# PEER in a hybrid block: gathered activations for block 2, and a dense product that ends ahead of the loop

## The chip, the cores and the metric

The kernel runs on one core of a Trainium2 chip. The metric is the device time of the whole program in microseconds (us), as the median of several executions.

## The reference, cut to what matters

One layer for 512 tokens of width 1024, all in float32: a projection, sparse attention, a chunked DeltaNet and a merge give x. Then comes PEER, a mixture of 16384 experts of one neuron each, of which every token takes 8 heads x 16 = 128:

```
h2 = rms_norm(x, norm2_gain)
q = h2 @ w_query                          # 8 heads x 2 x 128
s = q . sub_keys                          # 2 x 128 scores a head
expert, best = top 16 of the 16 x 16 sums of the two top-16 lists
gate = softmax(best)
act[n, hk] = gelu(u[expert[n, hk]] . h2[n])
x[n] += sum over hk of gate[n, hk] * act[n, hk] * v[expert[n, hk]]
```

Tables u and v have 16384 rows of 1024 numbers each. An expert's number is 128 times its first key plus its second.

## The kernel before, in words

PEER handles the tokens in four blocks of 128. Block 3 (GATHERED) follows the formula: `gathered(s)` for s = 0 to 127 fetches, for each of the block's tokens, the row of its expert s by an indirect DMA on POOL (`uv` holds u and v side by side, so a row is 8 KB and one gather 1 MB), multiplies its u half with the token's h2 and sums it on DVE (L960), takes Gelu and gate on ACT, and adds the v half times that number to `x1g` on DVE (L963).

Blocks 0 to 2 (WHOLE, 384 columns) compute the activations of all 16384 experts instead. `dense_u(i)` takes tile i, 128 experts: it loads `ut` (512 KB), splits it into two fp32r parts, `uh` (a cast on ACT, L167) and `ul` (a subtraction on DVE, L168), and multiplies them with the two parts of h2 transposed (`hT`): 8 times three matmuls (`mm3`, L91) of 384 columns. Gelu goes on ACT. 42 of the results are spilled, each stored to DRAM (L819) and loaded again later (`gs`); the others stay (`ge`).

`choose(b)` picks block b's experts and gates on DVE. `spread(b)` turns them into gate matrices, an expert by token: for 8 tokens at a time DVE compares a row of numbers with the first keys (`oa`, one instruction, L983) and, token by token, with the second keys, times the gate (`ob`, L986); PE multiplies the two one-hot matrices of each token (`wo<-oa,ob`, two matmuls for one fp32 product); ACT copies the results into `gb` (L992); and for 16 tokens (TC) at a time 1 MB is stored to `gd` in DRAM, in pieces of 8 KB. There are 24 such stores.

In the last loop `dense_v(i)` takes tile i of table v: load `vt` (512 KB), split it (`vh` on ACT L1044, `vl` on DVE L1045), multiply the activations into the gates of the tile (`gt`, L1046; gates are loaded for 8 tiles (IC) at a time, 1.5 MB in pieces of 512 B), split the product into `ch` and `cl`, and add 6 x 2 x 3 / 2 = 18 matmuls of 512 columns into six accumulators (`acc`).

Each engine, and SP for its DMA queue, works through its instructions in one fixed order. That order comes from the program's text: 62 tiles of the dense product are put among `choose` and `spread`, by the count of pieces of `spread` that are done, and 66 in the loop, about one behind every second `dense_v`; 6 of block 3's gathers come early, and 122 follow in the loop in proportion to the work that was issued.

## Time and profile before

| | |
|---|---|
| median of 3 runs | 1843.3 us (1842.14 to 1844.12) |
| the profiled execution | 1844.26 us |
| its span in the trace | 1842.5 us |
| PE, DVE, ACT, POOL busy | 1791.8, 1442.0, 803.1, 188.6 us |
| DMA traffic | 396.74 MB |

The span runs from the first to the last instruction that the trace shows; the execution's own time has 1.8 us more. The stages, in the trace's own time: up to 680 us all that precedes PEER's choice, to 1028 us the choice and the gate products (the last `wo<-oa,ob` ends there), then the loop. PE is TensorE's matmuls, and their busy time is not the same as work at its peak; "DMA share" is the mean busy share of the core's 16 DMA engines.

### The profile page before, as it was taken

What the parts mean: (1) busy time and instruction counts of PE and PEld (TensorE: products, weight loads), DVE (VectorE), ACT (ScalarE), POOL (GpSimd) and SP (SyncE); (2) the same over time, 40 slices, a digit from 0 to 9 for tenths busy, and PEclk for the clock granted to TensorE, in tenths of its full rate; (3) what the DMA queues carried; (4) which work ended last, traced back from release to release, by engine and by line L of the source; (5) the groups of instructions that cost most, each with busy time, mean ns of one, the idle gap of its engine ahead of it and who ended that gap; (6) DMA issues with size and microseconds to landing.
All of it is one profiled execution on the core that took longest, in us unless ns stands there. A gap on an engine that the chain in (4) does not pass through costs nothing.

```text
span 1842.5 us, 26292 instructions
## 1 busy us (share of the span) xinstructions
PE 1791.8 (97%) x9527; PEld 1572.5 (85%) x9527; DVE 1442.0 (78%) x3291; ACT 803.1 (44%) x1401; POOL 188.6 (10%) x132
## 2 busy tenths in 40 slices
PE   5999999999999999999999999999999999999998
PEld 4787677878788899999999988888888888888887
DVE  5767988654667899999997686788787887787886
ACT  5433434443533334555655444344443444343442
POOL 0000000000000000010000112122121222212220
PEclk9999999999999999999999999999999999999999
DMA  4211111111643214567676898989988988898974
GB/s 148 92 64 63 58 41 58 52 52 41 211 147 130 89 52 142 186 226 258 250 268 228 307 365 305 336 316 361 337 313 327 347 315 309 335 357 313 343 299 170
DMA packets 142354, 396.74 MB, mean 215 GB/s; under 512 B 10704, under 2 KB 71760, under 8 KB 122768
## 3 DMA queue, kind: packets, MB, share of 16 engines
q1 hardware_dynamic: 123792, 260.84, 40.3%
...
## 4 chain that ended last, share of the span: by engine, by line
PE 82%; DVE 8%; DMA 6%; ACT 2%; issue 1%; SPq 0%; DVEq 0%; ACTq 0%
PE mm L91 28%; PE acc L91 25%; PE wo L91 6%; PE dn L91 5%; PE at L91 3%; DMA vt<-in_uv_dram 2%; DMA gt<-gd 2%; DVE ul L168 1%; DVE ob L986 1%; PE tr L91 1%; PE at L571 0%; PE dn L320 0%; DMA wt<-in_w_br_dram 0%; DVE tmp L229 0%; DVE gt L1046 0%
## 5 line engine op out<-in xcount | busy, mean ns | idle before, releaser
L91 PE MATMUL acc<-vl,ch 128*128 128x512 f32 x768 | 299.5, 390 | 1.1 <-DVE vl L1045 1.1
L91 PE MATMUL acc<-vh,cl 128*128 128x512 f32 x768 | 298.2, 389 | 0.0
L91 PE MATMUL acc<-vh,ch 128*128 128x512 f32 x768 | 263.1, 390 | 4.9 <-ACT vh L1044 4.9
L951 POOL DMA_INDIRECT row<-in_uv_dram,eidx x124 | 178.6, 1441 | 832.3 <-DVE x1g L963 775.1
L167 ACT CAST uh<-ut 128x1024 fp32r<-128x1024 f32 x128 | 134.6, 1051 | 150.0 <-PE mm L91 84.0
L1045 DVE TENSOR_TENSOR vl<-vt,vh 128x1024 fp32r<-128x1024 f32 x128 | 156.4, 1222 | 50.3 <-ACT vh L1044 47.6
L168 DVE TENSOR_TENSOR ul<-ut,uh 128x1024 fp32r<-128x1024 f32 x128 | 155.9, 1219 | 34.4 <-ACT uh L167 33.8
L91 PE MATMUL mm<-hTh,uh 128*128 128x384 f32 x496 | 168.6, 340 | 2.9 <-ACT gs L818 1.9
L91 PEld LDWEIGHTS acc<-vh,ch 128*128 128x128 f32 x768 | 143.3, 188 | 32.1 <-ACT vh L1044 6.6
L91 PE MATMUL mm<-hTh,ul 128*128 128x384 f32 x496 | 168.0, 340 | 2.7 <-DVE ul L168 2.7
L91 PEld LDWEIGHTS acc<-vl,ch 128*128 128x128 f32 x768 | 144.2, 188 | 30.2 <-DVE vl L1045 2.1
L963 DVE SCALAR_TENSOR_TENSOR x1g<-row,co,x1g 128x1024 f32<-128x1024 f32 x128 | 163.8, 1280 | 7.4 <-ACT co L962 5.3
L91 PEld LDWEIGHTS acc<-vh,cl 128*128 128x128 f32 x768 | 144.1, 188 | 29.2
L1044 ACT CAST vh<-vt 128x1024 fp32r<-128x1024 f32 x128 | 133.9, 1046 | 78.4 <-DMA vt<-in_uv_dram 64.0
L91 PE MATMUL mm<-hTl,uh 128*128 128x384 f32 x496 | 167.3, 337 | 0.0
L167 ACT CAST ch<-gt 128x384 fp32r<-128x384 f32 x128 | 65.5, 512 | 218.1 <-PE acc L91 211.1
L960 DVE CUSTOM_DVE_ANT_0 scr<-row,h2g 128x1024 f32<-128x1024 f32 x128 | 156.0, 1218 | 0.3
L91 PE MATMUL mm<-hh,wh 128*128 128x512 f32 x344 | 144.6, 424 | 3.6 <-ACT hh L167 2.1
L168 DVE TENSOR_TENSOR wl<-wt,wh 128x1024 fp32r<-128x1024 f32 (+1 forms) x81 | 90.1, 1115 | 63.4 <-ACT wh L167 63.2
L91 PE MATMUL mm<-hh,wl 128*128 128x512 f32 x344 | 137.3, 401 | 0.0
L91 PE MATMUL mm<-hl,wh 128*128 128x512 f32 x344 | 136.9, 398 | 0.0
L167 ACT CAST wh<-wt 128x1024 fp32r<-128x1024 f32 (+1 forms) x81 | 77.7, 962 | 110.9 <-PE mm L91 86.7
...
## 6 DMA issues: line engine op xcount, KB each, us to landing
ut<-in_uT_dram SPq DMA_DIRECT2D x128, 512.0 KB
vt<-in_uv_dram SPq DMA_DIRECT2D x128, 512.0 KB
...
sgd<-tmp SPq DMA_DIRECT2D x16, 256.0 KB
```

The costliest lines, as they stand in the source:

```text
L91: hop[0] = PE.matmul(o, l, r, start=start, stop=stop).ins
L167: S.copy(hi, src)
L168: return V.tensor_tensor(lo, src, hi.bitcast(F32), op=ALU.subtract).ins
L951: G.indirect_dma_start(out=row.rearrange("p t d -> p (t d)"), out_offset=None, in_=uv, in_offset=bass.IndirectOffsetOnAxis(ap=released.get ...
L960: V.tensor_tensor_reduce(scr, row[:, 0], h2g, 1.0, 0.0, op0=ALU.mult, op1=ALU.add, accum_out=a)
L963: V.scalar_tensor_tensor(x1g, row[:, 1], co, x1g, op0=ALU.mult, op1=ALU.add)
L986: V.tensor_scalar(ob[:, t], io, sl[:, 1, n:n + 1], sl[:, 2, n:n + 1], op0=ALU.is_equal, op1=ALU.mult)
L1044: S.copy(vh, vt)
L1045: paced = V.tensor_tensor(vl, vt, vh.bitcast(F32), op=ALU.subtract)
```

## The change

Block 2 (HALF) leaves the dense product, which keeps blocks 0 and 1 and so 256 columns. Its activations come from gathers of the u halves alone: `ask(s)` fetches 128 rows of 4 KB, and `products()` multiplies and sums them with the block's h2 on DVE, into one column of `act` each, 128 in all. Then Gelu runs over `act` and is multiplied into block 2's gates ahead of `spread(2)`, so that in the loop only the gates of blocks 0 and 1 are multiplied by activations. The V product keeps all three blocks.

All 128 tiles of the dense product now come ahead of the loop, placed by a running count of costs (`along`). 48 of them (i % 8 in NATIVE) go to PE unsplit: fp32 products straight from `ut` and an fp32 copy of h2 transposed (`hTf`), with no cast and no subtraction. Activations are stored and loaded in groups of four tiles, 28 of the 32 groups of 512 KB each. `ob` is one comparison for 8 tokens, as `oa` is, and the gate is multiplied in by ACT, token by token. `gd` is written in pieces of 512 B and read in pieces of 12 KB. 16 gathers of block 3 come early, beside `spread(2)`, and 112 stay in the loop. There are three `vt`.

```diff
-WHOLE, GATHERED = (0, 1, 2), 3
-NU = len(WHOLE) * P
+DENSE, HALF, GATHERED = (0, 1), 2, 3
+WHOLE = DENSE + (HALF,)
+NU = len(DENSE) * P
...
-AHEAD = 20
-KEPT = 42
-SPILLED = {i for i in range(P) if i * KEPT // P != (i + 1) * KEPT // P}
-EARLY = 6
-HEAD = 4, 4
-EARLY_FROM, EARLY_TO = 6, 20
+GE = 4
+ONCHIP = {0, 8, 16, 24}
+NATIVE = (1, 4, 6)
...
     def dense_u(i, a_):
-        ut = up.tile([P, 8, P], F32, name="ut", bufs=2)
+        ut = uw.tile([P, 8, P], F32, name="ut", bufs=2)
         load(ut, uT[i])
-        uh = up.tile([P, 8, P], F32R, name="uh", bufs=2)
-        ul = up.tile([P, 8, P], F32R, name="ul", bufs=2)
-        split(uh, ul, ut)
-        for k in range(8):
-            mm3(a_, (uh[:, k, :], ul[:, k, :]), (hT[0][:, k, :NU], hT[1][:, k, :NU]), k == 0, k == 7)
-        if i in SPILLED:
...
-            nc.sync.dma_start(gsd[i], ge)
+        if i % 8 in NATIVE:
+            for k in range(8):
+                mm(a_, ut[:, k, :], hTf[:, k, :], k == 0, k == 7)
         else:
-            ges[i] = up.tile([P, NU], F32, name="ge", bufs=AHEAD + 2)
-            S.activation(ges[i], a_, AF.Gelu)
+            uh = uw.tile([P, 8, P], F32R, name="uh", bufs=2)
+            ul = uw.tile([P, 8, P], F32R, name="ul", bufs=2)
+            split(uh, ul, ut)
+            for k in range(8):
+                mm3(a_, (uh[:, k, :], ul[:, k, :]), (hT[0][:, k, :NU], hT[1][:, k, :NU]), k == 0, k == 7)
+        g, r = divmod(i, GE)
+        if r == 0:
+            if g in ONCHIP:
+                ges[g] = up.tile([P, GE, NU], F32, name="ge", bufs=len(ONCHIP))
+            else:
+                ges[g] = up.tile([P, GE, NU], F32, name="gs", bufs=2)
+        S.activation(ges[g][:, r], a_, AF.Gelu)
+        if r == GE - 1 and g not in ONCHIP:
+            gsd[g] = dr.tile([P, GE * NU], F32, name=f"gs{g}")
+            nc.sync.dma_start(gsd[g], ges.pop(g).rearrange("p r n -> p (r n)"))
...
-    released = {}
+    uv2 = uv.rearrange("e (t d) -> (e t) d", t=2)
+    asked = []
+    def ask(s):
+        if s % 2 == 0:
+            asked.append(rowq.tile([P, 2, D], F32, name="row", bufs=ROWS))
+        G.indirect_dma_start(
+            out=asked[s // 2][:, s % 2],
+            out_offset=None,
+            in_=uv2,
+            in_offset=bass.IndirectOffsetOnAxis(ap=eidh[:, s:s + 1], axis=0),
+        )
+    def products():
+        for s in range(AHEAD):
+            ask(s)
+        for s in range(P):
+            if s + AHEAD < P:
+                ask(s + AHEAD)
+            r = asked[s // 2][:, s % 2]
+            V.tensor_tensor_reduce(r, r, h2h, 1.0, 0.0, op0=ALU.mult, op1=ALU.add, accum_out=act[:, s:s + 1])
+            yield
...
-    gd = dr.tile([NCH, P, P * TC], F32, name="gd")
+    gd = dr.tile([P // IC, P, NCH, IC * TC], F32, name="gd")
...
                 oa = gp.tile([P, TB, P], F32, name="oa", bufs=2)
                 ob = gp.tile([P, TB, P], F32, name="ob", bufs=2)
-                rows_ = sl[:, 0, n0:n0 + TB, None].to_broadcast([P, TB, P])
-                paced = V.tensor_tensor(oa, io[:, None].to_broadcast([P, TB, P]), rows_, op=ALU.is_equal)
+                for i, o_ in enumerate((oa, ob)):
+                    which = sl[:, i, n0:n0 + TB, None].to_broadcast([P, TB, P])
+                    V.tensor_tensor(o_, io[:, None].to_broadcast([P, TB, P]), which, op=ALU.is_equal)
                 for t in range(TB):
                     n = n0 + t
-                    V.tensor_scalar(ob[:, t], io, sl[:, 1, n:n + 1], sl[:, 2, n:n + 1], op0=ALU.is_equal, op1=ALU.mult)
+                    S.activation(ob[:, t], ob[:, t], AF.Copy, scale=sl[:, 2, n:n + 1])
...
-            nc.sync.dma_start(gd[b * (P // TC) + c], gb.rearrange("p i n -> p (i n)"))
-            yield paced
+            dst = gd[:, :, b * (P // TC) + c, :].rearrange("g p k -> p g k")
+            nc.sync.dma_start(dst, gb.rearrange("p (g i) n -> p g (i n)", i=IC))
+            yield
...
+    uw = pool(gx, "uw", reuse_waits="tile")
     gp = pool(gx, "gp", reuse_waits="tile")
-    todo = list(first)
-    def dense(left):
-        while len(todo) > left:
+    todo = list(range(P))
+    total_c = NB * C_CHOOSE + NCH * C_PIECE + P + EARLY * C_SUM
+    spent_c = [0]
+    def along(cost):
+        spent_c[0] += cost
+        while len(todo) > LAST and (P - len(todo)) * total_c < spent_c[0] * (P - LAST):
             dense_u(todo.pop(0), bank("mm")[:, :NU])
...
+    of_half, done_h = products(), 0
+    def some(n):
+        for _ in range(n):
+            if next(of_half, 0) is None:
+                along(1)
+    along(C_CHOOSE)
+    choose(HALF)
+    along(C_CHOOSE)
+    choose(GATHERED)
+    some(8)
     n, slot = 0, 0
-    dense(len(first) - HEAD[0])
-    choose(GATHERED)
-    dense(len(first) - HEAD[0] - HEAD[1])
-    rest = len(todo)
-    for b in WHOLE:
+    for b in DENSE:
+        along(C_CHOOSE)
         choose(b)
-        for paced in spread(b, gp):
+        some(8)
+        for _ in spread(b, gp):
             n += 1
-            dense(rest * (NCH - n) // NCH)
-            with tc.issue_after(paced.ins):
-                if len(released) < min(ROWS, EARLY):
-                    s = len(released)
-                    released[s] = rowq.tile([P, 1], I32, name="free", bufs=ROWS)
-                    V.tensor_copy(released[s], eidx[:, s:s + 1])
-                while slot < EARLY and slot * (EARLY_TO - EARLY_FROM) < (n - EARLY_FROM) * EARLY:
-                    gathered(slot)
-                    slot += 1
+            along(C_PIECE)
+            some((P - 24) * n // 16 - (P - 24) * (n - 1) // 16)
+    some(P)
+    S.activation(act, act, AF.Gelu)
+    V.tensor_tensor(flat(gate[HALF]), flat(gate[HALF]), act, op=ALU.mult)
+    for i, _ in enumerate(spread(HALF, gp)):
+        along(C_PIECE)
+        while slot * 8 < (i + 1) * EARLY:
+            gathered(slot)
+            along(C_SUM)
+            slot += 1
+    while todo:
+        dense_u(todo.pop(0), bank("mm")[:, :NU])
     gx.close()
     rx.close()
...
+    load_gates(0)
...
-        if i % IC == 0:
-            gt[0] = ex.tile([P, NCH, IC, TC], F32, name="gt", bufs=2)
-            load(gt[0].rearrange("p c i n -> p c (i n)"), gd.rearrange("c p k -> p c k")[:, :, i * TC:(i + IC) * TC])
-        g = gt[0][:, :, i % IC, :]
-        vt = ex.tile([P, D], F32, name="vt", bufs=2)
...
+        if i % IC == 1 and i + IC < P:
+            load_gates(i // IC + 1)
+        g = gts[i // IC][:, :, i % IC, :]
+        vt = ex.tile([P, D], F32, name="vt", bufs=3)
...
-        V.tensor_tensor(g, activations(i).rearrange("p (c n) -> p c n", n=TC), g, op=ALU.mult)
+        gdn = g[:, :ND]
+        V.tensor_tensor(gdn, activations(i).rearrange("p (c n) -> p c n", n=TC), gdn, op=ALU.mult)
...
-    late = fresh[AHEAD:]
-    total_u = len(late)
-    total = P * V_COST + total_u * U_COST
-    spent, slot = 0, EARLY
     for i in range(P):
         paced = dense_v(i)
-        spent += V_COST
-        if late and (total_u - len(late)) * (P - END) <= i * total_u:
-            dense_u(late.pop(0), ps3.tile([P, NU], F32, name="a_", bufs=2))
-            spent += U_COST
         with tc.issue_after(paced.ins):
-            while (slot - EARLY) * total < spent * (P - EARLY) and slot < P:
+            while (slot - EARLY) * P < (i + 1) * (P - EARLY) and slot < P:
                 gathered(slot)
                 slot += 1
     xs = [rowq.tile([P, 2, D], F32, name="xs", tag="row", bufs=ROWS)[:, 0] for b in WHOLE]
```

The order on DVE, where the last gate matrices give way to the loop. Before (`ul` belongs to a dense tile, `oa` and `ob` to the gates, and `gt`, `cl`, `vl` are the loop's first tile):

```order
L168 TENSOR_TENSOR ul<-ut,uh 128x1024 x2
L983 TENSOR_TENSOR oa<-io,sl 128x1024
L986 TENSOR_SCALAR ob<-io,sl 128x128 x8
L983 TENSOR_TENSOR oa<-io,sl 128x1024
L986 TENSOR_SCALAR ob<-io,sl 128x128 x8
L168 TENSOR_TENSOR ul<-ut,uh 128x1024 x4
L1046 TENSOR_TENSOR gt<-ge,gt 128x24x16 x6
L168 TENSOR_TENSOR cl<-gt,ch 128x384 x2
L1045 TENSOR_TENSOR vl<-vt,vh 128x1024
```

In the changed kernel, at the same place:

```order
L172 TENSOR_TENSOR ul<-ut,uh 128x1024
L1024 TENSOR_TENSOR oa<-io,sl 128x1024
L1024 TENSOR_TENSOR ob<-io,sl 128x1024
L172 TENSOR_TENSOR ul<-ut,uh 128x1024 x36
L1115 TENSOR_TENSOR gt<-ge,gt 128x16x16 x4
L1115 TENSOR_TENSOR gt<-gs,gt 128x16x16 x4
L172 TENSOR_TENSOR cl<-gt,ch 128x384 x2
L1112 TENSOR_TENSOR vl<-vt,vh 128x1024
L1000 ISA row,a<-row,h2g 128x1024
```

Behind the last `ob` there were 4 subtractions of dense tiles and then the loop; now there are 36. On PE, 53 dense tiles (33 split, 20 unsplit) now stand between the last `wo<-oa,ob` and the first `acc`, where 3 or 4 stood; of 80 split tiles 44 have their `ul` ahead of the last `ob`, where 60 had it before.

The order of SP's DMAs from the last stores of gates (`gd<-gb`) to the first tiles of table v (`vt`); `gs_9799<-gs` and its like are stores of spilled activations, `gs<-gs_6319` loads of them. Before:

```order
L819 DMA gs_9834<-gs 128x384
L102 DMA ut<-in_uT_dram 128x1024
L993 DMA gd<-gb 128x2048
L102 DMA gt<-gd 128x24x128
L102 DMA vt<-in_uv_dram 128x1024
L819 DMA gs_9917<-gs 128x384
L102 DMA vt<-in_uv_dram 128x1024
L102 DMA ut<-in_uT_dram 128x1024
L102 DMA gt<-gd 128x24x128
L819 DMA gs_9952<-gs 128x384
L102 DMA ut<-in_uT_dram 128x1024
```

In the changed kernel the last `gd<-gb` stands 44 loads of `ut` ahead of these rows:

```order
L838 DMA gs_11210<-gs 128x1024
L106 DMA ut<-in_uT_dram 128x1024 x4
L838 DMA gs_11395<-gs 128x1024
L106 DMA ut<-in_uT_dram 128x1024 x2
L106 DMA gs<-gs_6498 128x1024
L106 DMA gt<-gd 128x3072
L838 DMA gs_11494<-gs 128x1024
L106 DMA vt<-in_uv_dram 128x1024
L106 DMA gt<-gd 128x3072
L106 DMA vt<-in_uv_dram 128x1024 x2
```

The loads of `ut` went on among those of `vt` for the whole loop; now all of them come first, and the first `vt` is behind the store of the last group of activations.

## Rows read from the trace of the kernel before

**Rows 1.** Parts 1 (busy time) and 4 (chain that ended last) of the page.

```profile
span 1842.5 us, 26292 instructions
...
PE 1791.8 (97%) x9527; PEld 1572.5 (85%) x9527; DVE 1442.0 (78%) x3291; ACT 803.1 (44%) x1401; POOL 188.6 (10%) x132
...
PE 82%; DVE 8%; DMA 6%; ACT 2%; issue 1%; SPq 0%; DVEq 0%; ACTq 0%
```

**Rows 2.** Busy time by stage; last three columns: TensorE clock, DMA share, GB/s.

```profile
0.00:680.00 680.00, 647.06 (x3400) 523.29 (x3401) 475.61 (x1497) 280.16 (x523) 0.20 (x4) 0.99 0.25 86
680.00:940.00 260.00, 254.42 (x1646) 252.74 (x1645) 254.43 (x826) 142.30 (x185) 15.97 (x9) 1.00 0.60 212
940.00:1028.00 88.00, 88.00 (x598) 88.00 (x597) 65.98 (x150) 50.10 (x63) 1.68 (x1) 1.00 0.65 235
1028.00:1842.50 814.50, 802.36 (x3889) 708.42 (x3887) 646.03 (x821) 330.55 (x632) 170.77 (x118) 1.00 0.88 322
```

**Rows 3.** Pieces of the chain that ended last: start, length, what.

```profile
976.24 3.57 PE wo L91 x32
...
1028.80 4.62 DMA gs<-gs
...
1441.42 8.16 PE acc L91 x36
1449.58 4.19 PE a__13633 L91 x24
...
1825.20 11.80 PE acc L91 x52
```

**Rows 4.** Groups by line and form: busy us, mean ns of one.

```profile
L168 DVE TENSOR_TENSOR ul<-ut,uh 128x1024 fp32r<-128x1024 f32 x128 | 155.9, 1219 | 34.4 <-ACT uh L167 33.8 <-PE a__11289 L91 0.3
...
L167 ACT CAST uh<-ut 128x1024 fp32r<-128x1024 f32 x128 | 134.6, 1051 | 150.0 <-PE mm L91 84.0 <-PE wo L91 7.1 <-DVE bp L894 4.5
...
L986 DVE TENSOR_SCALAR ob<-io,sl 128x128 f32<-128x128 f32 x384 | 102.8, 343 | 0.0
L91 PE MATMUL wo<-oa,ob 128*128 128x128 f32 x768 | 96.3, 275 | 0.0
...
L992 ACT COPY gb<-wo 128x512 f32<-128x512 f32 x96 | 94.4, 1088 | 51.2 <-DMA gd<-gb 32.6 <-PE wo L91 14.7 <-PE mm L91 3.7
...
L983 DVE TENSOR_TENSOR oa<-io,sl 128x1024 f32<-128x1024 f32 x48 | 58.5, 1219 | 3.9 <-PE wo L91 3.9
```

**Rows 5.** Timeline of DVE, 1443 to 1448 us: start, us, what.

```profile
1443.22 1.22 DVE L960 CUSTOM_DVE_ANT_0 scr<-row,h2g 128x1024 f32<-128x1024 f32 x1
...
1444.36 1.28 DVE L963 SCALAR_TENSOR_TENSOR x1g<-row,co,x1g 128x1024 f32<-128x1024 f32 x1
1445.56 1.22 DVE L168 TENSOR_TENSOR ul<-ut,uh 128x1024 fp32r<-128x1024 f32 x1
1446.70 0.55 DVE L1046 TENSOR_TENSOR gt<-ge,gt 128x384 f32<-128x384 f32 x1
1447.16 0.55 DVE L1046 TENSOR_TENSOR gt<-gs,gt 128x384 f32<-128x384 f32 x1
1447.63 1.28 DVE L963 SCALAR_TENSOR_TENSOR x1g<-row,co,x1g 128x1024 f32<-128x1024 f32 x1
```

**Rows 6.** Timeline of PE, 150 to 151 us.

```profile
150.00 0.70 PE L91 MATMUL at<-ikT,iqT 64*128 64x256 f32 x2
150.63 0.50 PE L91 MATMUL mm<-hh,wh 128*128 128x512 f32 x1
```

**Rows 7.** DMA queues from 1028 to 1830 us: packets, MB, share of 16 engines.

```profile
q1 hardware_dynamic: 83073, 136.14, 48.6%
q0 software_dynamic: 16992, 123.74, 39.6%
```

**Rows 8.** A stretch of 20 us in the loop, columns as in Rows 2.

```profile
1240.00:1260.00 20.00, 20.00 (x101) 17.99 (x100) 18.57 (x26) 8.89 (x17) 4.52 (x4) 1.00 1.01 401
```

**Rows 9.** Waits of DVE: us in total, times, longest.

```profile
DVE gt L1046 <- DMA gt<-gd: 43.9, 10, 8.7
```

More of the change, by code (lines that the diff above doesn't have):

```diff
@@ L187, in tile_block @@
         mm(hs(rb, tb), r1[:, tb:tb + 1].to_broadcast([P, P]), ident)
-    rbs = pp.tile([P, T], F32, name="rbs")
+    rbs = tmp()
     S.copy(rbs, rb)
@@ L686, in tile_block @@
     h2g = lp.tile([P, D], F32, name="h2g")
+    h2h = lp.tile([P, D], F32, name="h2h")
+    hTf = lp.tile([P, 8, NU], F32, name="hTf")
     hT = tuple(lp.tile([P, 8, T], F32R, name=f"hT{n}") for n in "hl")
@@ L718, in second_norm @@
         r2 = mp.tile([P, 1], F32, name="r2", bufs=2)
-        h = h2g if b == GATHERED else mp.tile([P, D], F32, name="h2t", bufs=2)
+        h = (h2h, h2g)[b % 2]
         S.activation(h, x1[b], AF.Square, accum_out=s1)
@@ L790, in tile_block @@
     eidx = xp.tile([P, P], I32, name="eidx")
+    eidh = xp.tile([P, P], I32, name="eidh")
+    act = xp.tile([P, P], F32, name="act")
     rx, qx, wx = ExitStack(), ExitStack(), ExitStack()
@@ L807, in dense_u @@
     def dense_u(i, a_):
-        ut = up.tile([P, 8, P], F32, name="ut", bufs=2)
+        ut = uw.tile([P, 8, P], F32, name="ut", bufs=2)
         load(ut, uT[i])
-        uh = up.tile([P, 8, P], F32R, name="uh", bufs=2)
-        ul = up.tile([P, 8, P], F32R, name="ul", bufs=2)
-        split(uh, ul, ut)
-        for k in range(8):
-            mm3(a_, (uh[:, k, :], ul[:, k, :]), (hT[0][:, k, :NU], hT[1][:, k, :NU]), k == 0, k == 7)
-        if i in SPILLED:
-            ge = up.tile([P, NU], F32, name="gs", bufs=2)
-            gsd[i] = dr.tile([P, NU], F32, name=f"gs{i}")
-            S.activation(ge, a_, AF.Gelu)
-            nc.sync.dma_start(gsd[i], ge)
-        else:
-            ges[i] = up.tile([P, NU], F32, name="ge", bufs=AHEAD + 2)
-            S.activation(ges[i], a_, AF.Gelu)
-    def activations(i):
-        if i in ges:
-            return ges.pop(i)
-        ge = up.tile([P, NU], F32, name="gs", bufs=2)
-        load(ge, gsd[i])
-        return ge
-    fresh = [i for i in range(P) if i not in SPILLED]
-    first = sorted(fresh[:AHEAD] + list(SPILLED))
+        if i % 8 in NATIVE:
+            for k in range(8):
+                mm(a_, ut[:, k, :], hTf[:, k, :], k == 0, k == 7)
+        else:
+            uh = uw.tile([P, 8, P], F32R, name="uh", bufs=2)
[13 more added lines that the diff above has]
+            nc.sync.dma_start(gsd[g], ges.pop(g).rearrange("p r n -> p (r n)"))
+    def activations(i):
+        g, r = divmod(i, GE)
+        if g not in ges:
+            ges[g] = up.tile([P, GE, NU], F32, name="gs", bufs=2)
+            load(ges[g].rearrange("p r n -> p (r n)"), gsd[g])
+        return ges[g][:, r]
     ts = [rp.tile([P, 2, 8, 16], F32, name=f"ts{b}") for b in range(NB)]
@@ L932, in choose @@
             V.tensor_tensor(sel[b][part], by_h(oh[:, 0]), by_h(oh[:, 1]), op=ALU.add)
+        if b == HALF:
+            ef = rp.tile([P, 8, 16], F32, name="ef")
+            V.tensor_scalar(ef, sel[b][1], 2.0, None, op0=ALU.mult)
+            V.scalar_tensor_tensor(eidh.rearrange("p (h k) -> p h k", k=16), sel[b][0], 256.0, ef, op0=ALU.mult, op1=ALU.add)
         if b == GATHERED:
@@ L954, in gathered @@
             in_=uv,
-            in_offset=bass.IndirectOffsetOnAxis(ap=released.get(s, eidx[:, s:s + 1]), axis=0),
+            in_offset=bass.IndirectOffsetOnAxis(ap=eidx[:, s:s + 1], axis=0),
         )
@@ L958, in gathered @@
         co = rowq.tile([P, 1], F32, name="co", bufs=3)
-        scr = rowq.tile([P, D], F32, name="scr", bufs=1)
-        V.tensor_tensor_reduce(scr, row[:, 0], h2g, 1.0, 0.0, op0=ALU.mult, op1=ALU.add, accum_out=a)
+        V.tensor_tensor_reduce(row[:, 0], row[:, 0], h2g, 1.0, 0.0, op0=ALU.mult, op1=ALU.add, accum_out=a)
         S.activation(co, a, AF.Gelu)
```

14 lines of the change are left out of this document (11 added, 3 removed).

## The prediction

> **What bounds the kernel now.** The page first: PE is busy 1791.8 of 1842.5 us, DVE 1442.0, and the chain that ended last is 82% PE [rows 1]. A share of the whole span says little about a change in two stages, so the same numbers by stage come next [rows 2]. Up to 680 us (projection, attention, DeltaNet, merge) nothing is touched. From 680 to 1028 us, the gate stage, PE and DVE are both full: 254.42 and 254.43 us busy of the first 260, with the DMA engines at 0.60 to 0.65. From 1028 us on, the loop, PE is busy 802.36 of 814.5 us, DVE 646.03, and the DMA engines already 0.88. In the chain the dense product and the V product take turns on PE, one tile of 24 matmuls after 36 of the V product [rows 3]: so in the loop a microsecond taken off PE is a microsecond gained only until the DMA engines' 0.88 becomes 1.
>
> The profiled execution took 1844.26 us, 1.8 more than its span, and stands 0.05% above the median of 1843.3. I sum stages on its time axis and add the 1.8.
>
> **Prices.** On PE, one of the two matmuls of an fp32 product of 128 columns takes 3.57/32 = 0.1116 us; a split (fp32r) matmul takes 4.19/24 = 0.1746 with 384 columns and 8.16/36 = 0.2267 with 512 [rows 3]. The 0.0521 per 128 columns between the two, taken off once more, gives 0.1225 for 256 columns: a split tile of 24 costs 2.94 us (half of 0.2267 is the lower bound: 2.72). An unsplit tile is 8 fp32 products of 256 columns, which no row shows with 128 partitions. From below: twice the gate product's pace, 4 x 0.1116 = 0.446, so 3.57 us a tile. From above: the fp32 product of 256 columns with 64 partitions, 0.63 us from its start to the next [rows 6], so 5.04. I take 3.57, since the gate product has the same operands' shape on the array. On DVE I use the step from one start to the next [rows 5]: multiply-and-sum over 1024 columns 1.14, multiply-add into x1g 1.20, ul 1.14 (oa and vl have the same form), a tile of 384 columns 0.47, and by the line between 384 and 1024 columns 0.34 for 256.
>
> **The gate stage, on DVE.** Before: 254.43 + 65.98 = 320.4 us busy [rows 2]. Removed: 384 ob's, 102.8 us [rows 4]. Added: 48 compares of the form of oa for ob, 48 x 1.14 = 54.7; the 128 multiply-and-sums with the half rows, 128 x 1.14 = 145.9. Moved: by the two orders of DVE 60 ul's stood ahead of the last ob and 44 do now, -16 x 1.14 = -18.2; 16 gathered pairs instead of 6, 10 x 2.34 = +23.4. Sum 423.4; at the 254.43/260 that DVE reaches now, 433 us. PE needs about 327 here (48 split tiles, 28 unsplit, 768 gate matmuls: 141 + 100 + 86; a tile at the edge is counted twice), so DVE, not PE, sets this stage. The 384 scalings go to ACT. It was busy 142.30 + 50.10 = 192.4 us of this stage [rows 2], 94.4 of them for the gb's [rows 4], so 433 leave it about 240: the scalings are hidden there unless one costs over 0.6 us.
>
> Transfers in the same stage: 75 ut's of 0.52 MB (39.3), half rows 67.1, early gathers 16.8, gd 25.2, spilled activations 8.4: 156.8 MB. What the DMA engines carry when full is 401 GB/s at a share of 1.01 [rows 8]; by queue, SP's moved 136.14 MB in 48.6% of 802 us, 349 GB/s, and the gather queue 123.74 MB in 39.6%, 390 GB/s [rows 7]. The 156.8 MB need 391 us by the one, 73/349 + 84/390 = 424 us by the others. DVE and DMA are then both full, and the half rows all lie in the first two thirds, since block 2's gates wait for the last of them: there some 117 MB want about 316 us, as much as DVE's own work. Two such streams don't fit into each other without loss; I add a tenth, 32 us (bounds: nothing with DVE at its sum of 423, and twice as much). The stage ends at 680 + 433 + 32 = **1145 us** (1103 to 1177).
>
> **The tail of dense tiles.** In the changed kernel's order 53 dense tiles, 33 split and 20 unsplit, stand on PE behind the last gate product and ahead of the first V product; nothing else is there, and DVE has only 36 ul's to do (the two orders above). PE's work: 33 x 2.94 + 20 x 3.57 = 168 us (161 with 2.72, 198 with 5.04). An unsplit tile gives its ut back only when PE is done with it, and there are two ut's: the next load (4.62 us for a load of a spilled tile, [rows 3]), a cast of 1.05 on ACT [rows 4] and 1.14 for ul must fit beside one tile of 2.94. Where the tile that comes to the freed buffer is a split one (two of three times) it is up to 3.9 us late, else up to 1.7: 0 to 63 us for the 20. I take about half, 30: the 4.62 was measured with the DMA engines near full, and here they are mostly free. The tail is **198 us** (161 to 261) and ends at 1343. Before, this work cost the loop 66 x 4.19 = 277 us of PE, so the tail alone is no loss; the loss is that DVE, the gathers and the vt loads, which ran under those 277 us, stand still meanwhile.
>
> **Into the loop.** On SP the first vt stands behind the last store of activations, which waits for the last tile's Gelu: a load, a cast, a subtraction, some 8 us, which is also the longest wait for gates now, 8.7 [rows 9]. The loop starts at 1351.
>
> **The loop.** PE: 128 x 18 x 0.2267 = 522 us. DVE: 128 x (1.14 + 0.47 + 0.34) + 112 x 2.34 = 512. Transfers: vt 67.1, gathers 117.4, gt 25.2, spilled activations 14.7, x1 1.6: 226 MB, 564 us at 401 GB/s, 301 + 311 = 612 by the queues' rates. (Now 260 MB have 814 us.) So here the DMA engines end last, and PE has to wait. gt now comes in pieces of 12 KB instead of 512 B, which speaks for more than 349 GB/s on SP's queue; three streams near their limits speak for less than 401. I take the middle, **588 us** (564 to 612). The loop ends at 1939; the last sums and stores take 1842.5 - 1837.0 = 5.5 [rows 3].
>
> Sum: 1343 + 8 + 588 + 5.5 = 1944.5, with the 1.8 **1946 us**, 5.6% above 1843.3.
>
> **The rivals.**
> *The loop goes at PE's pace* (the DMA engines carry the 226 MB in time): 522 us at PE's 802.36/814.5 is 530, 58 less: 1888. For it: gt's long pieces. Against it: 226/530 is 426 GB/s, over the 401 at a share of 1.01. The Trainium skill (HBM Reference, Specifications) says that a core which streams alone measures about 425 GB/s, held by its 16 DMA engines; by that the loop would take an estimated 532 us. No stretch of this trace reaches that; the 401 was measured with gathers and 512-byte pieces among the transfers.
>
> *The tail is dearer*: unsplit tiles at 5.04 us and the load latencies in full, 261 us in place of 198: 2009. For it: the only row with 256 fp32 columns. Against it: it has another shape on the array.
>
> *Faster: the transfers never bind.* With no loss to transfers in the gate stage (433), loads early enough in the tail (168) and the loop at 530, the end is 680 + 433 + 168 + 8 + 530 + 7.3 = 1826. It decides once 107 of the 120 us that I charge to transfers (32 + 30 + 58) are gone. For it: no stage of the kernel before waited for bandwidth, so its ceiling isn't proven. Against it: the shares of 1.01 [rows 8] and 0.88 over the whole loop [rows 2].
>
> *Faster: the time follows PE's work.* The dense product falls from 128 x 4.19 = 536 to 80 x 2.94 + 48 x 3.57 = 407 us; if PE stayed at its 97%, the end would be 130 us earlier: 1714. The orders speak against it: nothing lies beside the 53 tiles for DVE. The Trainium skill (Perfetto Trace Analysis, Identifying the Most-Contended Engine) has one find the engine with the highest occupancy and optimize that first, which by these rows is PE, and would give that 1714. The same page (Optimization Strategy) says that where the most-contended engine changes over time, interleaving those regimes may help; this change takes such an interleaving apart, and the stage rows agree, with PE at 98.5% and DVE at 79% of the loop now [rows 2].
>
> **Chances.** Forecast 0.58 (its own range 1900 to 1985: one bound at a time), loop at PE's pace 0.18, dearer tail 0.15, transfers never bind 0.07, time follows PE 0.02. The range of 1870 to 2020 leaves out the last two (0.09), the upper half of the dearer tail (0.07) and little else. The last two rivals end below; 0.2%, about what a measurement of this kernel can tell from no change, is 3.7 us, and of the 0.07 around 1826 some 0.01 falls within it. So faster 0.08, same 0.01, slower 0.91.
>
> **What the changed profile would show.** Right: to about 1145 us DVE busy over 90% and PE near 70%, the DMA share near 1 up to two thirds of it; then some 200 us with PE alone, DVE under 30% and POOL idle; then a loop of 560 to 610 us with the DMA share at 1, PE near 89% and waiting for vt, and DVE near 87%. Unsplit matmuls show 3.57 us for a tile or 5.04. Wrong: a loop at PE over 97%; a gate stage under 433 us; dense tiles that run without gaps; or a clock that falls. It is 1.00 in all stages from 680 us on, where PE never was under 97% busy [rows 2]; with waits in the gate stage and the loop that is not assured, and at the lower of the two levels (1.2 GHz) the tail's 168 us would double.

## The result, and the profile after

The changed kernel takes 1982.4 us (median of 4, 1973.7 to 1992.5) against 1843.7 before: a ratio of 1.0736 with a 95% interval of 1.07 to 1.0772. It is slower, as forecast, and by 7.4% where 5.6% was forecast; 1982.4 lies between 1870 and 2020. The profiled execution has a span of 1986.5 us.

The page of the changed kernel (busy time, two of the lines in 40 slices of about 50 us, and the chain that ended last), to be read beside [rows 1]:

```profile
span 1986.5 us, 25813 instructions
...
PE 1746.0 (88%) x9143; PEld 1476.7 (74%) x9143; DVE 1472.5 (74%) x3162; ACT 865.7 (44%) x1742; POOL 389.8 (20%) x260
...
PEclk9999999999999997788877899999899999999999
DMA  4211011115422269999999865545999999999998
...
PE 53%; DMA 19%; DVE 16%; ACT 7%; issue 4%; SPq 0%; DVEq 0%; ACTq 0%
```

PE's busy time fell by 45.8 us, DVE's rose by 30, and the span rose by 144. The chain is 53% PE where it was 82%, and DMA has 19% of it. The TensorE clock, at 9 in every slice before, is lower in slices 16 to 23, from the half rows to the middle of block 2's gates, and in slice 29.

By stage, from the first multiply-and-sum of a half row (734.5), the first gate product (834.2), the last half row (1033.3), the last gate product (1204.7) and the first V product (1408.0) to the last (1980.8); columns as in [rows 2]:

```profile
734.50:834.20 99.70, 52.62 (x253) 46.07 (x251) 99.62 (x290) 17.19 (x27) 65.49 (x49) 0.75 0.96 350
834.20:1033.30 199.10, 146.67 (x893) 137.78 (x894) 181.85 (x263) 133.16 (x310) 117.63 (x77) 0.83 0.97 345
1033.30:1204.70 171.40, 140.89 (x912) 132.58 (x912) 104.93 (x108) 121.01 (x285) 26.43 (x17) 0.90 0.81 274
1204.70:1408.00 203.30, 173.28 (x1114) 159.20 (x1113) 42.70 (x43) 55.38 (x91) 0.00 (x0) 0.96 0.53 189
1408.00:1980.80 572.80, 541.54 (x2303) 439.57 (x2304) 519.77 (x714) 238.14 (x477) 173.51 (x108) 0.97 0.97 383
```

| stage | forecast | measured | difference |
|---|---|---|---|
| gate stage ends at | 1145 | 1204.7 | +59.7 |
| tail and start of the loop | 206 | 203.3 | -2.7 |
| loop | 588 | 572.8 | -15.2 |
| end | 5.5 | 5.7 | +0.2 |

In the order of the rows: while the half rows come, DVE is busy 281.5 of 298.8 us and the DMA engines at 0.96 and 0.97, PE far less. In the gates of block 2 (1033.3 to 1204.7 us) nothing is full: PE is busy 140.89 of 171.4, DVE 104.93, DMA 0.81. In the tail POOL is idle, DVE at 21%, DMA at 0.53. In the loop the DMA engines are at 0.97. The half rows end at 1033.3, where the forecast's terms add up to 680 + 316 + 32 = 1028; block 2's gates take 171.4 us, where the forecast left 1145 - 1028 = 117. So 54 of the 60 us are lost there.

What PE waits for in the loop, and ACT for PE's sake (total, times, longest):

```profile
ACT co L1001 <- DVE a L1000: 76.0, 60, 2.9
PE acc L95 <- ACT vh L1111: 38.7, 18, 7.9
ACT vh L1111 <- DMA vt<-in_uv_dram: 32.9, 34, 3.6
```

PE waits for vh, and vh in its turn for vt. ACT, which works in one fixed order, also stands 76.0 us before `co`, for DVE's sums over the gathered rows. By queue in the loop (POOL's gathers are q0, SP's queue q1):

```profile
q0 software_dynamic: 15552, 113.25, 49.6%
q1 hardware_dynamic: 24879, 105.60, 47.2%
```

That is 113.25 MB in 49.6% of 572.8 us, 399 GB/s, and 105.60 MB in 47.2%, 391 GB/s; before it was 390 and 349 [rows 7]. The same two queues while the half rows came (734.5 to 1033.3 us):

```profile
q0 software_dynamic: 18538, 69.05, 63.2%
q1 hardware_dynamic: 30324, 34.20, 33.1%
```

69.05 MB in 63.2% of 298.8 us are 366 GB/s, less than the 399 of whole rows in the loop. The length of the rows is not shown to be the reason: in the first half of block 2's gates (1033.3 to 1120 us) whole rows moved at 350 GB/s, and in e6 below half rows at 384.

The prices on PE. An unsplit tile (8 products, 16 matmul instructions) and the matmul behind it, in the tail:

```profile
1246.02 3.69 PE L95 MATMUL mm<-hTf,ut 128*128 128x256 f32 x16 [0.44 <-ACT gs L835]
1249.36 0.47 PE L95 MATMUL mm<-hTh,uh 128*128 128x256 f32 x1
```

An unsplit tile took 1249.36 - 1246.02 = 3.34 us (3.57 forecast), a split one 24 x 0.118 = 2.83 by the same timeline (2.94). And 8 gate products in block 2's gates, with the row of that stretch (columns as in [rows 2]):

```profile
1103.50:1107.50 4.00, 3.66 (x17) 3.66 (x18) 2.57 (x2) 3.83 (x5) 3.12 (x3) 0.50 0.71 245
1103.84 3.78 PE L95 MATMUL wo<-oa,ob 128*128 128x128 f32 x16 [4.07 <-ACT gb L1033]
```

They took 3.57 us to the next matmul (at 1107.41), 0.223 for an instruction, twice the 0.1116 of [rows 3]: the granted clock there was 0.50, the lower level (1.2 GHz), behind a wait of 4.07 us for ACT. Of the new DVE and ACT work the groups by line say:

```profile
L986 DVE CUSTOM_DVE_ANT_0 row<-row,h2h 128x1024 f32<-128x1024 f32 x128 | 153.4, 1223 | 4.2 <-DMA row<-in_uv_dram,eidh 4.2
...
L1027 ACT ACTIVATE ob<-ob,sl 128x128 f32<-128x128 f32 x384 | 117.8, 391 | 37.7 <-DVE ob L1024 37.7
```

The chain in the tail, 1236 to 1254 us:

```profile
1236.44 6.33 PE mm L95 x38
1242.79 4.33 DMA ut<-in_uT_dram
...
1247.19 1.05 ACT uh L171
...
1248.27 1.24 DVE ul L172
1249.52 3.48 DMA ut<-in_uT_dram
...
1253.08 1.05 ACT uh L171
```

A load of ut, its cast, its subtraction, then the next load into the same buffer: this round, 6.7 and 5.9 us here, comes between PE's pieces.

### The profile page after: what moved, and what is told of

It is laid out like the page before. It is cut to its first block, busy times and chain, and to the rows that moved or that the text cites. A ratio compares the mean times of both kernels' runs of the same rounds, so it can differ in the third digit from the quotient of the medians.

```text
span 1986.5 us, 25813 instructions
## 1 busy us (share of the span) xinstructions
PE 1746.0 (88%) x9143; PEld 1476.7 (74%) x9143; DVE 1472.5 (74%) x3162; ACT 865.7 (44%) x1742; POOL 389.8 (20%) x260
## 4 chain that ended last, share of the span: by engine, by line
PE 53%; DMA 19%; DVE 16%; ACT 7%; issue 4%; SPq 0%; DVEq 0%; ACTq 0%
PE mm L95 24%; PE acc L95 15%; DMA vt<-in_uv_dram 8%; DMA ut<-in_uT_dram 7%; PE dn L95 5%; PE wo L95 4%; DVE row L986 4%; DMA gd<-gb 3%; PE at L95 3%; DVE ul L172 3%; ACT gb L1033 2%; ACT uh L171 2%; DVE vl L1112 1%; DVE x1g L1003 1%; DVE ob L1024 1%
## 5 line engine op out<-in xcount | busy, mean ns | idle before, releaser
L971 POOL DMA_INDIRECT row<-in_uv_dram,eidh x128 | 184.7, 1443 | 833.5 <-PE mm L95 725.7
L95 PE MATMUL mm<-hTh,uh 128*128 128x256 f32 x640 | 198.9, 311 | 47.0 <-ACT uh L171 43.9
L95 PE MATMUL acc<-vh,ch 128*128 128x512 f32 x768 | 205.0, 404 | 38.7 <-ACT vh L1111 38.7
L95 PE MATMUL mm<-hTh,ul 128*128 128x256 f32 x640 | 196.7, 308 | 47.7 <-DVE ul L172 47.7
L95 PE MATMUL mm<-hTl,uh 128*128 128x256 f32 x640 | 189.9, 297 | 0.0
L95 PE MATMUL mm<-hTf,ut 128*128 128x256 f32 x768 | 181.4, 391 | 7.5 <-DMA ut<-in_uT_dram 5.7
L95 PEld LDWEIGHTS mm<-hTh,uh 128*128 128x128 f32 x640 | 132.7, 207 | 55.5 <-ACT uh L171 50.5
L95 PEld LDWEIGHTS mm<-hTh,ul 128*128 128x128 f32 x640 | 131.9, 206 | 54.4 <-DVE ul L172 53.8
L95 PEld LDWEIGHTS mm<-hTf,ut 128*128 128x128 f32 x768 | 147.2, 196 | 28.5 <-issue 5.7
L986 DVE CUSTOM_DVE_ANT_0 row<-row,h2h 128x1024 f32<-128x1024 f32 x128 | 153.4, 1223 | 4.2 <-DMA row<-in_uv_dram,eidh 4.2
L1000 DVE CUSTOM_DVE_ANT_0 row<-row,h2g 128x1024 f32<-128x1024 f32 x128 | 155.6, 1217 | 0.8 <-DMA row<-in_uv_dram,eidx 0.8
```

The costliest lines, as they stand in the source:

```text
L95: hop[0] = PE.matmul(o, l, r, start=start, stop=stop).ins
L971: G.indirect_dma_start(out=asked[s // 2][:, s % 2], out_offset=None, in_=uv2, in_offset=bass.IndirectOffsetOnAxis(ap=eidh[:, s:s + 1], axi ...
L986: V.tensor_tensor_reduce(r, r, h2h, 1.0, 0.0, op0=ALU.mult, op1=ALU.add, accum_out=act[:, s:s + 1])
L1000: V.tensor_tensor_reduce(row[:, 0], row[:, 0], h2g, 1.0, 0.0, op0=ALU.mult, op1=ALU.add, accum_out=a)
```

## The experiments

All times are medians beside the kernel before on the same chip (1843 to 1849); those of e6, e7, e8 and e11 are one execution each. "Half rows" is where the last of them is summed, "gates" from there to the last gate product, "tail" to the first V product. The loop, whose work the edits of e2, e4 and e6 to e9 leave as it is, took 564 to 589 us in them; so a difference of less than 25 us in that column says little.

| run | half rows end | gates | tail | loop | time |
|---|---|---|---|---|---|
| the change | 1033 | 171 | 203 | 573 | 1982.4 |
| e1, 52 tiles in the loop | 1032 | 172 | 23 | 708 | 1932.1 |
| e2, ob's gate on DVE | 1044 | 159 | 203 | 564 | 1980.2 |
| e3, gd in pieces of 8 KB | 1019 | 167 | 203 | 615 | 2016.0 |
| e4, four ut | 1069 | 192 | 31 | 589 | 1891.5 |
| e5, no early gathers | 1031 | 202 | 157 | 610 | 2011.2 |
| e6, four ut, short sums | 1048 | 195 | 30 | 574 | 1853.7 |
| e7, four ut, no half rows | 1147 | 77 | 17 | 571 | 1818.4 |
| e8, four ut, all split | 1085 | 177 | 46 | 572 | 1887.9 |
| e9, four ut, tail kept | 1063 | 125 | 169 | 572 | 1938.8 |
| e10, four ut, 28 early | 1076 | 207 | 29 | 580 | 1892.8 |
| e11, four ut, 56 gathers fewer | 1072 | 188 | 30 | 535 | 1832.1 |
| e12, four ut, six vt | 1069 | 190 | 30 | 532 + 109 | 1932.2 |

**e1: tiles back into the loop.** The pool of ut, uh and ul stays open, and group 24 is spilled as well.

```diff
+LATE, END = 52, 8
-    todo = list(range(P))
+    todo = list(range(P - LATE))
+    late = list(range(P - LATE, P))
...
         paced = dense_v(i)
+        while late and (LATE - len(late)) * (P - END) <= i * LATE:
+            dense_u(late.pop(0), ps3.tile([P, NU], F32, name="a_", bufs=2))
```

> The last 52 tiles of the dense product go back into the loop, about one behind every second or third tile of the V product; everything ahead of the last gate product stays as in the changed kernel. Theory of the stages (each stretch has its own bound, and in the tail only PE works): the gate stage ends at about 1205 us as before, the tail of 203 us shrinks to some 15, the loop grows from 573 us to PE's 522 + 164 = 686 at 98%, about 700; end near 1930, some 50 us less. Rival, PE's work alone counts: the tail's 173 us of PE work move and the end moves by under 20 us. Rival, the clock: with PE fuller the granted clock in the loop returns to 1.00 and the whole gain is the clock's; then the stretch to 1205 us, whose clock is the lowest, shows nothing.

Measured 1932.1 us (ratio 1.0463, 1.0401 to 1.0524). Gates of block 2, tail and loop:

```profile
1031.90:1203.40 171.50, 135.06 (x854) 125.93 (x855) 105.57 (x109) 121.63 (x294) 28.33 (x17) 0.88 0.80 268
1203.40:1226.30 22.90, 15.68 (x92) 14.48 (x90) 5.12 (x10) 6.49 (x11) 0.00 (x0) 0.85 0.94 313
1226.30:1934.20 707.90, 687.86 (x3352) 581.30 (x3352) 559.85 (x748) 281.52 (x558) 162.36 (x108) 0.99 0.94 357
```

As the theory of the stages had it (1930, and a loop of about 700): the loop takes 707.9 us with PE busy 687.86 of it, so here PE is the bound again and the transfers (0.94) are hidden. The gate stage ends at 1203.4 us with its low clock unchanged, and all of the gain lies behind it, which the clock's rival had said too; it falls by size. Behind the gates PE was busy 173.28 + 541.54 us in the change and 15.68 + 687.86 here: 11 us less, with one tile more, so a higher clock can have given some 15 us of PE's work, while that stretch got 45 us shorter (776.1 to 730.8).

**e2: the gate in ob by DVE again.**

```diff
-                for i, o_ in enumerate((oa, ob)):
-                    which = sl[:, i, n0:n0 + TB, None].to_broadcast([P, TB, P])
-                    V.tensor_tensor(o_, io[:, None].to_broadcast([P, TB, P]), which, op=ALU.is_equal)
+                which = sl[:, 0, n0:n0 + TB, None].to_broadcast([P, TB, P])
+                V.tensor_tensor(oa, io[:, None].to_broadcast([P, TB, P]), which, op=ALU.is_equal)
                 for t in range(TB):
-                    S.activation(ob[:, t], ob[:, t], AF.Copy, scale=sl[:, 2, n:n + 1])
+                    V.tensor_scalar(ob[:, t], io, sl[:, 1, n:n + 1], sl[:, 2, n:n + 1], op0=ALU.is_equal, op1=ALU.mult)
```

> The gates of ob are multiplied in by DVE token by token again, as in the kernel before: DVE gets 384 instructions for 48 (102.8 us for 54.7), ACT loses its 384 scalings. Theory of the stages: until the last half row (1034 us) the DMA engines are full and DVE is not, so at most 20 us are lost there; in the gates of block 2 (1034 to 1205 us) a chain of DVE, ACT and PE sets the pace and is shorter without the scalings, so 15 to 40 us are won; in all 0 to 20 us less. Rival, DVE sets the gate stage (the prediction's step): 48 us more, near 2030.

Measured 1980.2 us (ratio 1.0729, 1.0644 to 1.0814), 2 us from the change:

```profile
829.30:1043.60 214.30, 153.65 (x964) 143.14 (x965) 200.82 (x436) 73.97 (x94) 111.94 (x77) 0.85 0.94 327
1043.60:1202.70 159.10, 127.91 (x841) 120.50 (x840) 128.55 (x273) 70.35 (x117) 27.92 (x17) 0.86 0.86 289
```

The half rows end 10 us later with DVE fuller, the gates take 12 us less. On balance DVE's 48 us more cost nothing and ACT's scalings won nothing; the run changes both at once and doesn't part them. In the gates DVE has 24 us more to do and the stretch is shorter, so the prediction's step by which DVE sets the whole gate stage is wrong for its last third.

**e3: gd's pieces.**

```diff
-    gd = dr.tile([P // IC, P, NCH, IC * TC], F32, name="gd")
+    gd = dr.tile([NCH, P, P * TC], F32, name="gd")
...
-            nc.sync.dma_start(dst, gb.rearrange("p (g i) n -> p g (i n)", i=IC))
+            nc.sync.dma_start(gd[b * (P // TC) + c], gb.rearrange("p i n -> p (i n)"))
```

The loads of `gt` are changed to match.

> Gates are stored in pieces of 8 KB and loaded in pieces of 512 B again, as in the kernel before. Theory: the gb's wait less for the stores (24.7 us of waits in the changed kernel, most of it on the path in the gates of block 2), so the gate stage ends 10 to 25 us earlier; the loop, where the DMA engines are full, gets the short pieces and loses 10 to 25 us; the end moves by under 15 us. Rival, the stores in short pieces are what makes the gate stage late: it ends near 1145 us, 60 us earlier, and the end with it.

Measured 2016.0 us (ratio 1.0922, 1.0826 to 1.1018):

```profile
1018.60:1185.10 166.50, 137.65 (x913) 129.77 (x912) 104.97 (x108) 121.12 (x285) 26.45 (x17) 0.90 0.77 283
...
1387.60:2002.20 614.60, 554.08 (x2303) 447.42 (x2304) 520.28 (x715) 237.54 (x477) 158.70 (x108) 0.94 0.97 357
```

The gate stage ends at 1185.1, 20 us earlier, within what was expected; the loop takes 614.6 us, 42 more, and that size was missed. SP's queue in this loop:

```profile
q1 hardware_dynamic: 67783, 105.85, 49.8%
```

105.85 MB in 49.8% of 614.6 us are 346 GB/s, against 391 with the long pieces: close to the 349 of [rows 7]. PE's wait for vh in the loop grew from 38.7 to 63.5 us, and vh's for vt from 32.9 to 69.6. So the new layout is worth 22 us to the change on balance (34 by the medians).

**e4: four ut.** `bufs=4` for `ut`, nothing else.

> Four ut instead of two, nothing else. Theory: in the tail the loads of ut, with two buffers, set the pace (load 4 us, cast 1.05, subtraction 1.24 in a chain); with four the tail goes at PE's 33 x 2.83 + 20 x 3.66 = 167 us, so 203 us shrink to about 175, and the last 40 us of the gate stage, where the same chain shows, by some 15: end near 1940. Rival, PE's work sets the tail and the loads are hidden: no change, 1975 to 1990.

Measured 1891.5 us (ratio 1.0248, 1.0164 to 1.0332), 91 less where some 40 were expected:

```profile
830.30:1069.10 238.80, 201.10 (x1345) 186.91 (x1343) 204.25 (x284) 149.96 (x342) 127.42 (x86) 0.96 0.99 360
1069.10:1261.20 192.10, 170.21 (x1174) 160.74 (x1175) 116.94 (x118) 133.21 (x306) 27.11 (x17) 0.95 0.87 298
1261.20:1291.70 30.50, 21.99 (x148) 20.56 (x146) 6.21 (x13) 8.35 (x15) 0.00 (x0) 0.91 0.69 235
1291.70:1880.40 588.70, 540.41 (x2304) 434.47 (x2304) 518.50 (x714) 237.59 (x477) 174.28 (x108) 0.99 0.96 372
```

The tail is 30.5 us long. The order says why this is not only latency: with four ut 121 dense tiles stand on PE ahead of the last gate product and 7 behind it, with two it was 75 and 53. The text of the program places 124 tiles among the gates either way, so the order does not come from the text alone, as it was put ahead of the prediction: with two buffers it was made with 53 tiles pushed back. That unsplit tiles, which hold a ut to PE's end, are the reason is argued and not shown, as no run here has two ut and no unsplit tile. Ahead of the loop the four ut win 116 us (1408.0 to 1291.7); the loop took 16 more.

**e9: the two effects of e4 apart.** Four ut, and the matmuls of the last 53 tiles held behind the last gate product.

```diff
-LAST = 4
+LAST = 53
...
+    held[0] = wo_last[0]
     while todo:
         dense_u(todo.pop(0), bank("mm")[:, :NU])
```

with `with behind(held[0]):` around the matmuls of `dense_u`.

> Four ut, but the last 53 dense tiles are held behind the last gate product on PE, 33 split and 20 unsplit as in the changed kernel; only their loads may come earlier. This parts the two things that four ut's change. Theory, the place of the 53 tiles is the cost: the tail falls from 203 us only to PE's 33 x 2.83 + 20 x 3.66 = 167 and some 10 to the loop, the stretch ahead of it stays near 1205 us, end 1940 to 1965. Rival, the loads' latency is the cost and their place is none: end near the 1890 of four ut's in free order.

Measured 1938.8 us (ratio 1.0485, 1.0373 to 1.0597):

```profile
1063.30:1187.90 124.60, 66.24 (x354) 62.87 (x354) 84.68 (x91) 92.88 (x238) 26.23 (x17) 0.69 0.78 256
1187.90:1357.10 169.20, 162.61 (x1116) 154.14 (x1114) 41.75 (x42) 55.16 (x91) 0.00 (x0) 0.99 0.63 215
```

With loads in time the tail takes 169.2 us, PE busy 162.61: 34 us of the 203 were loads that came late. Another 47 us separate this run from e4 (65 ahead of the loop, whose own time differs by 17): those are the place of the tiles, PE alone where DVE and the gathers could have worked. The first row holds a second finding. In block 2's gates there is now no dense tile at all, and they take 124.6 us. But the same 75 tiles stand ahead of the last gate product, now all before the last half row, and the half rows end 30 us later (1063.3): the gate stage as a whole ends only 17 us earlier than in the change.

**e5: no early gathers.** `EARLY = 0`.

> The changed kernel with none of block 3's gathers beside the gates of block 2: all 128 in the loop. In the order 40 dense tiles are left behind the last gate product instead of 53. Theory: the 16 early gathers fill the DMA engines in the first half of block 2's gates (1033 to 1120 us at a share near 1) and hold them up; without them that stretch of 171 us falls to 150 or less, though it holds 13 more dense tiles; the tail falls from 203 to 40 x 3.8 = 153 us; the loop, full of transfers, grows by 16.8 MB at 383 GB/s, 44 us; end near 1955 (1940 to 1970). Rival, block 2's gates are held up by the chain of DVE, ACT and PE alone: the stretch stays at 171 us or grows, and the end is near 1980 or above.

Measured 2011.2 us (ratio 1.0904, 1.0873 to 1.0936); the gates of block 2 and the tail:

```profile
1031.20:1232.70 201.50, 173.33 (x1164) 161.52 (x1162) 79.58 (x70) 130.64 (x286) 1.68 (x1) 0.94 0.62 199
1232.70:1389.50 156.80, 132.28 (x842) 120.98 (x840) 32.93 (x35) 42.81 (x70) 0.00 (x0) 0.95 0.56 191
```

The theory fell, and the rival's numbers came: without gathers and at a DMA share of 0.62 the gates take 201.5 us. What grew is the number of dense tiles among them, counted by their matmuls in that stretch: 0 in e9 (124.6 us), 26.7 in the change (171.4), 38.7 here (201.5), 38.9 in e4 (192.1). e4 and e9 have the same ut and gathers, so a dense tile that stands on PE between the gate products costs that stretch about (192.1 - 124.6)/38.9 = 1.7 us. What the gathers cost there is not parted: e5 has none, but its casts wait 45.3 us for loads of ut, of which it has two; e10, with 12 gathers more than e4 and the same tiles, takes 15 us longer.

**e6 and e7: DVE's work and the bytes of the half rows, one at a time.** Both with four ut. In e6 the sums run over 64 of 1024 columns; in e7 all 128 sums use the first half row.

```diff
-            V.tensor_tensor_reduce(r, r, h2h, 1.0, ...
+            V.tensor_tensor_reduce(r[:, :64], r[:, :64], h2h[:, :64], 1.0, ...
```

```diff
-            if s + AHEAD < P:
-                ask(s + AHEAD)
-            r = asked[s // 2][:, s % 2]
-            V.tensor_tensor_reduce(r, r, h2h, 1.0, ...
+            r = asked[0]
+            V.tensor_tensor_reduce(r[:, 1], r[:, 0], h2h, 1.0, ...
```

> Four ut, and the multiply-and-sum over each half row cut to 64 of its 1024 columns (block 2's activations are then not the reference's): DVE loses some 130 us, all transfers stay. In the run with four ut the half rows took from 732 to 1069 us. Theory, transfers set that stretch: it stays within 25 us of 337. Rival, DVE sets it (302 us busy of 337): it falls by 100 us or more.

Measured 1853.7 us. The second part of the half rows (from the first gate product), and the loop:

```profile
782.80:1047.60 264.80, 222.96 (x1511) 207.55 (x1512) 130.99 (x337) 164.89 (x374) 115.98 (x104) 0.96 1.01 374
...
1272.50:1846.20 573.70, 540.87 (x2303) 439.75 (x2304) 519.86 (x715) 238.03 (x477) 175.82 (x108) 0.98 0.98 382
```

> Four ut, and only the first half row fetched, which all 128 multiply-and-sums use (block 2's activations are then not the reference's): 66.5 MB of transfers fewer, all work of DVE stays. Theory, transfers set the stretch of the half rows: it falls from 337 us to DVE's 302 or a little more, and the end by 30 to 50 us; the loop stays at 589. Rival, DVE sets it: the stretch and the end stay within 15 us of 1886.

Measured 1818.4 us. The second part of the stretch with the sums, the gates, and the loop:

```profile
880.90:1146.50 265.60, 255.83 (x1843) 243.45 (x1842) 240.11 (x323) 193.08 (x424) 6.94 (x3) 0.99 0.70 229
1146.50:1223.60 77.10, 58.36 (x380) 56.20 (x379) 40.09 (x37) 68.26 (x168) 0.94 (x1) 0.87 0.49 150
...
1240.30:1810.80 570.50, 539.46 (x2303) 439.01 (x2304) 520.17 (x717) 237.64 (x477) 169.52 (x108) 0.98 0.97 383
```

Without 130 us of DVE's work the half rows take 316.6 us instead of 336.8, at a DMA share of 1.01 in the part shown: the transfers set this stretch, as expected of the theory. Without the bytes the stretch did not fall to 302 us, as the theory had it, but grew to 409.7: the order filled it with dense tiles (105, where e4 has 64), PE is busy 255.83 of its last 265.6 us, and the gates behind it fell to 77, with 255 gate matmuls instead of 351, 6 tiles and no gather in them. The end comes 73 us earlier than in e4, more than expected; 51 of them lie ahead of the loop and 18 in the loop, whose work is the same. This run is 1.4% below the kernel before, by one execution.

**e8: no unsplit tiles.** `NATIVE = ()`, with four ut.

> Four ut, and no unsplit tiles: 48 more casts (50 us of ACT) and subtractions (55 us of DVE), PE's dense product cheaper by 48 x 0.83 = 40 us. Theory, DVE and the transfers are full while the half rows come and PE is not: the end comes 15 to 45 us later than with unsplit tiles, 1900 to 1930. Rival, the unsplit tiles are too dear on PE: up to 40 us earlier, 1850.

Measured 1887.9 us, no change from e4, which neither side expected. Ahead of the loop it is 17 us later (1308.8 to 1291.7), as the theory had it, and the loop, with the same work, 17 us shorter; by one execution that stays open. Its second part of the half rows:

```profile
873.00:1085.00 212.00, 165.87 (x1185) 159.66 (x1184) 194.54 (x266) 152.97 (x339) 115.12 (x71) 0.89 0.96 338
```

The unsplit tiles are 24 us dearer on PE in all (48 x 0.5), not 40.

**e10 to e12: the loop.** With four ut each. e10 has `EARLY = 28`; e11 leaves out the last 56 gathers (`slot < 72`); e12 has six vt.

> Four ut, and 28 gathers of block 3 beside the gates of block 2 instead of 16, so 100 in the loop. Theory, the loop is set by transfers and block 2's gates are not (a share of 0.87 of the DMA engines there): the loop loses 12.6 MB at 372 to 383 GB/s, 33 us, block 2's gates gain 10 to 20 us, the end comes 10 to 25 us earlier than 1891. Rival, the gates' stretch gets all of it back: no change, within 8 us. A gain of over 48 us, which would bring it below the kernel before, is expected by neither.

Measured 1892.8 us (ratio 1.0236, 1.0106 to 1.0367), as the rival had it. Gates and loop:

```profile
1075.70:1282.90 207.20, 177.60 (x1175) 166.03 (x1176) 144.67 (x154) 136.42 (x329) 41.73 (x29) 0.93 0.94 338
...
1311.70:1891.50 579.80, 541.87 (x2304) 438.46 (x2304) 492.43 (x678) 228.80 (x453) 130.07 (x96) 0.98 0.93 356
```

> Four ut, and the last 56 of block 3's gathers left out with all their work (block 3 is then not the reference's): the loop keeps 56 of 112, so 167 MB instead of 226 and DVE about 380 us instead of 512. It is to tell what sets the loop, 572 to 589 us in the runs so far, where 100 gathers instead of 112 made it no shorter. Theory, transfers (with DVE close behind) set it: it falls to PE's 522 / 0.985 = 530 us and ACT's waits for vt are gone; end near 1835. Rival, a chain through vt, vh and PE sets it, whatever the DMA engines carry: it stays above 565 us.

Measured 1832.1 us. The loop:

```profile
1290.00:1824.70 534.70, 526.78 (x2304) 433.08 (x2304) 393.93 (x547) 206.67 (x365) 81.65 (x52) 1.00 0.83 300
```

> Four ut, and six vt instead of three in the loop; nothing else. In the run with four ut PE waited 54 us in the loop for ACT's vh, and vh in part for vt. Theory, the transfers set the loop: six buffers only ask earlier for the same bytes, the loop stays at 572 to 589 us and the end within 10 us of 1891. Rival, late vt's set it while the mean share of 0.96 leaves room: PE's waits fall by 30 us or more and the loop goes to 540 to 555 us, the end to 1850 to 1865, still above the kernel before.

Measured 1932.2 us (ratio 1.0472, 1.0427 to 1.0517). The loop, and the 108.8 us between the last V product and the end:

```profile
1289.20:1821.30 532.10, 525.46 (x2303) 433.05 (x2304) 445.78 (x615) 218.46 (x413) 105.64 (x79) 1.00 0.90 347
...
1821.30:1930.10 108.80, 0.44 (x2) 0.01 (x1) 82.43 (x103) 15.92 (x64) 45.75 (x30) 0.52 0.89 332
```

With half of the gathers the loop runs at PE's 534.7 us, as expected of transfers as its bound; but DVE's work is also less (393.93 us), and so is ACT's wait for it (16.2 us where e4 has 97.5), so this run alone doesn't part the two. e3 does more for transfers, with the same work and shorter pieces. e12 fits neither side: PE goes at its 532.1 us, but the gathers fall behind, and 108.8 us of nothing but them follow. The order on DVE changed with the buffers: in e4 the work of all 128 gathers stands ahead of the loop's last `vl`, in e12 that of 94. With fewer gathers beside it the loop's DMA share is 0.90, so nothing here shows that the vt's won bandwidth from the gathers. Why e10's loop, with 12 gathers fewer, is only 9 us shorter than e4's and no shorter than the others' is not settled: PE still waits for vh there 43.1 us, at a share of 0.93.

## Why the prediction was right, and where it was off

The mechanism of the forecast held in two of its three stages; the third was mis-sized beyond its own bounds. In part the total was luck: the tail and the loop, 18 us short, hid some of the 60 by which the gate stage was late.

**The tail** was forecast at 198 us and 8 to the loop, and took 203.3. Its terms hold one by one: PE's work 168, by e9 162.6 busy; late loads 30, by e9 34. An unsplit tile took 3.34 us, so the rival of the dearer tail (5.04) falls. The place of the tiles was read from the order rightly: e4, which takes them back among the gates by two more buffers, wins 91 us, of which e9 gives 47 to the place; e1, which takes them back into the loop, wins 50.

**The loop** was forecast at 588 us by the transfers and took 572.8 at a share of 0.97. The term was 15 us too large. SP's queue moved 391 GB/s instead of the 349 taken from the short pieces; e3, with the short pieces, has 346 and a loop 42 us longer. But 15 us is also within what the same loop differs by from run to run. The rival by which PE sets it would have been 530 us; it comes true only where gathers are taken away (e11) or put off (e12). The Trainium skill (HBM Reference, Specifications) puts a core that streams alone at about 425 GB/s; the loop's mean is 383, and the measurement decides.

**The gate stage** is the step that failed in size: "DVE, not PE, sets this stage", which gave 1145 us (1103 to 1177) where 1204.7 was measured. While the half rows came, DVE and the DMA engines were both near full, as forecast, and that part ended within 5 us of its sum; e6 shows that the DMA engines set it there. The half rows also moved at 366 GB/s where the sum used 390. But in block 2's gates neither was full. What the step overlooked is that PE's 327 us of work are no cover when they stand in one fixed order with the gate products: each dense tile there costs about 1.7 us (e4 against e9), so the 26.7 tiles come to 46 us in a stretch that is 54 over. This is the price of that place and not what another place would save: e9, with the same tiles ahead of the last half row, ends the stage only 17 us earlier. What the rest of the 60 us hangs on stays open. The clock fell too, which the prediction had named as a sign of being wrong: to 0.75, 0.83 and 0.90 in the rows of this stage, but only to 0.96 in the tail, whose price did not double. How much of the lateness is PE's lower clock, no run parts from the waits that go with it.

**The rivals.** PE's work fell and the time rose, so the time does not follow PE. Transfers do bind: the change with four ut gets below the kernel before only where bytes are left out, the half rows' in e7 (by 26 us) or those of 56 gathers in e11 (by 13), one execution each, although by the prices above the dense product fell from 536 us to 80 x 2.83 + 48 x 3.34 = 387. The Trainium skill (Perfetto Trace Analysis, Optimization Strategy) says that interleaving stretches with different bounds may help; e1, which puts tiles back among the V products, agrees, with 50 us.

No version here that computes everything beats the kernel before; the best, e8, e10 and e4, are 2.4 to 2.5% slower, e8 by one execution.
